# Dense expert queries taken straight from the score stage, gates multiplied in another order, and a transpose inside the RWKV inverse

## The chip, the cores and the metric

The kernel runs on one core of a Trainium2 chip. The metric is the device time of one execution in microseconds (us). The engines are named as the profile names them: PE (TensorE matmul), PEld (its weight loads), DVE (VectorE), ACT (ScalarE), POOL (GpSimd), SP (the queue that issues most DMAs).

## The reference, cut to what matters

A decoder block over 512 tokens of width 1024. After two token mixers (a gated short convolution and RWKV-7 heads) comes a product-key expert layer, PEER, in which each token picks 128 of 16,384 experts:

```python
def one_block(xb):                        # 128 tokens
    q = (xb @ wq).reshape(tb, HEADS, 2, HALF)
    s = einsum('thcd,hcnd->thcn', q, subkeys)
    sv, si = lax.top_k(s, 16)             # 16 of 128 keys, for each half
    ...                                   # 16 of the 256 sums: idx, top_s
    gate = softmax(top_s)
    hid = gelu(einsum('td,thkd->thk', xb, tab_u[idx]))
    return einsum('thk,thkd->td', gate * hid, tab_v[idx])
```

A second normalisation, a per-layer gate and a final normalisation follow. Everything is float32.

## The kernel before, in words

There are four tiles of 128 tokens, 0 to 3. A planner orders each engine's instructions by a rank (`rank(n)`, lower first) and by what is ready. Instructions given to `pin` keep the order in which the program lists them. Every engine executes its own list strictly in order.

**Group stages.** `group` runs the mixers, the query normalisation and the key scores, first for tile 0, then for tiles 1 to 3 together. Inside it, `rwkv` inverts a triangular matrix for each head. `inverse` does four heads at once in seven levels (`lv`), two chains beside each other. In a level, PE makes `Z` (L459) and `TT` (L466), DVE copies the blocks into `DT` (L468), and the transposed `Dm` is needed for the next level. At the low levels DVE transposes (L470); at the others, 32 times in all, PE multiplies `DT` by the even columns of the identity (L474) and ACT copies the 64 columns for each head into `Dm` (L476). The normalised queries of the group are written to `uq` (L226, called from `group`) and transposed for the product with `wq` (L629). For each of the 16 blocks of `wq` the weights and then a 64 KB block of subkeys `sk` are loaded on SP; `sk` has two buffers.

**Sparse tiles.** For tiles 0 and 1 each chosen expert row is fetched (POOL, `g`, 512 KB for each fetch, L768), first 128 rows of `peer_u` for the dot products (DVE, L795), then 128 rows of `peer_v` that are added to the result (DVE, L799). The rows go round in a ring of `RB = 5` buffers with the tag "g". 220 of the 256 fetches of tile 0 are spread over the group stage of tiles 1 to 3.

**Dense tiles.** For tiles 2 and 3 the kernel multiplies with all experts instead, in 128 blocks `j`. `turn_queries` makes the normalised queries again (`u2`, L226, in a buffer of the same ring "g"), PE transposes them (L892) and ACT copies them (L893). `products_of(j)` loads a block `U` (512 KB, L907) and makes 16 matmuls into PSUM (L910). `settle_block(j, gated)` applies Gelu and leaves the result in `w`. The first `J0 = 36` blocks are done with no gates. Meanwhile DVE, with POOL and ACT, selects the experts of tiles 1, 2 and 3 (`selection`, tiles `keys` and `sel`; `sel` lies in the place of `uq`). Then `Gates` turns the chosen numbers and gates (L969 to L976), and the loop over `j` from `J0` has 92 + 2 steps.

One step of that loop, in program order and all pinned: `rows_of` builds the one-hot rows of four tokens (DVE L982, L986; ACT L988 to L991); `rows(PA)` fetches and works about two sparse rows (`PA = 1.95`); `settle_block` settles block `j-1`; `joined` multiplies the one-hot rows that were built a step earlier (PE L996, into `cb`), and `placed` puts the product into `w`: blocks that are already settled are multiplied by it (DVE L1006), later ones get a copy (ACT L1008); last, `products_of(j)`. Of the 94 steps, 64 build and 64 join, spread evenly up to block `J1 = 125`. The heart of `settle_block` is

```python
if gated:
    held(act.activation(p[:, 0:gated], p[:, 0:gated], AF.Gelu_apprx_tanh))      # L919
    held(dve.tensor_tensor(w[:, 0:gated], w[:, 0:gated], p[:, 0:gated], op=OP.mult))   # L920
if gated < 256:
    held(act.activation(w[:, gated:256], p[:, gated:256], AF.Gelu_apprx_tanh))  # L922
```

**Values and end.** A last loop over 128 blocks multiplies `w` with blocks `V` of `peer_v` (PE L1073) beside the sparse rows that are left (`PB = 1.06` for each block); then come the per-layer gate and the output.

Of the kernel before, what the change touches and what calls it, by code (L numbers as in the profile page):

```python
# [9 lines left out]
F32 = mybir.dt.float32  # L10
# [5 lines left out]
AF = mybir.ActivationFunctionType  # L16
OP = mybir.AluOpType
# [3 lines left out]
T, D = 512, 1024  # L21
# [23 lines left out]
RB = 5  # L45
# [3 lines left out]
N1 = 60  # L49
N0 = 82  # L50
RA = 2.05
J0 = 36
J1 = 125
VS = 2
PA = 1.95
PB = 1.06
FIRST = 92
LEAD = 4
# [3 lines left out]
def tile_block(ctx: ExitStack, tc: tile.TileContext, x, smalls, bvec, w1, w2, wbr, wout, wq, wup, gup, subk,  # L62
               peer_u, peer_v, pT, plew, peer_ut, out, dbg=None):
    nc = tc.nc
    dve, act, pool, pe, sp = nc.vector, nc.scalar, nc.gpsimd, nc.tensor, nc.sync
# [7 lines left out]
    ring = ctx.enter_context(tc.tile_pool(name="ring", bufs=1))  # L73
# [17 lines left out]
    def rank(n):  # L91

        tc.cur_priority = int(100000 * n)
# [25 lines left out]
    ident = keep.tile([128, 128], F32, name="ident")  # L119
# [101 lines left out]
    def pin(ins):  # L221

        return tc.keep_in_program_order(ins)

    def queries_in(t, r, u):
        dve.scalar_tensor_tensor(u, hrows(t), r, gain, op0=OP.mult, op1=OP.mult)  # L226
        return u

    idx_t, gate_t, rs, ready = {}, {}, {}, []
# [13 lines left out]
    def group(tiles, wide, meanwhile=None):  # L243
        n = len(tiles)
        N = 128 * n
        stage = ExitStack()

        choice = ExitStack()
# [3 lines left out]
        wpool = stage.enter_context(tc.tile_pool(name="wpool", bufs=1, side="right", reuse_waits="tile"))  # L252
# [7 lines left out]
        def load_w(src, name, whole=wide):  # L260

            w = wpool.tile([128, KC, 128], F32, name=name, tag="w", bufs=WB[wide])
            sp.dma_start(w, src)
            if whole:
                return [w]
            place = [wpool.tile([128, KC, 128], F32R, name=f"w{q}", tag=f"w{q}", bufs=WH) for q in range(2)]
            return parts_of(w, *place)
# [42 lines left out]
        convT = big.tile([128, 4, N], F32, name="convT", tag="convT")  # L310
# [52 lines left out]
        def rwkv(i, t):  # L363
# [5 lines left out]
            p = rw_ps("d")  # L369
# [5 lines left out]
            kt = hp4("kt")  # L375
            ecol = work.tile([128, 4, 2], F32, name="ecol", tag="ecol", bufs=2)
            for hp in range(4):
                p = rw_ps("cs")
# [4 lines left out]
            a, kk, am = hp4("a"), hp4("kk"), hp4("am")  # L383
            p = rw_ps("ap")
# [6 lines left out]
            p = rw_ps("ks")  # L391
# [7 lines left out]
            p = rw_ps("rk")  # L399
# [16 lines left out]
            p = rw_ps("pb")  # L416
# [3 lines left out]
            p = rw_ps("pg")  # L420
# [4 lines left out]
            for name, src in (("b", bt), ("k", kt), ("v", v)):  # L425
                p = tr_ps("tk")
# [6 lines left out]
            for hd in range(NH):  # L433
                hp, e = divmod(hd, 2)
                q = slice(e * 64, e * 64 + 64)
                p = rw_ps("A")
# [6 lines left out]
            def inverse(g4):  # L443

                DT, Dm = hp4("DT", f"DT{g4}"), hp4("Dm", f"Dm{g4}")
                made = act.activation(DT, ident[:, None, :].to_broadcast([128, 4, 128]), AF.Copy)
                if not wide:
                    tc.keep_in_program_order(made)
                final[g4] = DT
                for lv in range(7):  # L450

                    part = lambda ap, odd: ap.rearrange("p (b two c) -> p b two c", two=2, c=1 << lv)[:, :, odd, :]
                    pairs = lambda ap, odd: ap.rearrange("p h (b two c) -> p (h b) two c", two=2, c=1 << lv)[:, :, odd, :]
                    packed = lambda p: p[:, 0:256].rearrange("p (a c) -> p a c", c=1 << lv)

                    m = 64 if lv == 6 else 128
                    p = rw_ps("Z")
                    for q in range(4):
                        pe.matmul(p[:m, q * 64:(q + 1) * 64], lhsT=AT[:, g4 * 4 + q, 3, :m], rhs=part(DT[:, q, :], 1), start=True, stop=True)  # L459
                    yield  # L460
                    if lv:
                        Z = hp4("Z", "Z", 2)[:, 0:2].rearrange("p a (b c) -> p (a b) c", c=64)
                        act.activation(Z[:m], p[:m, 0:256].rearrange("p (a b) -> p a b", b=64), AF.Copy)
                        p = rw_ps("TT")
                        for q in range(4):
                            pe.matmul(p[:m, q * 64:(q + 1) * 64], lhsT=Dm[:m, q, :m], rhs=Z[:m, q, :], start=True, stop=True)  # L466
                        yield
                    dve.copy_predicated(pairs(DT, 1)[:m], lmask[:m, lv].rearrange("p (a c) -> p a c", c=1 << lv), packed(p)[:m])  # L468
                    if lv < BLOCKT[wide]:
                        dve.transpose(flat(Dm), flat(DT))  # L470
                    elif lv < 6:
                        p = rw_ps("DD")
                        for q in range(4):
                            pe.matmul(p[:, q * 64:(q + 1) * 64], lhsT=DT[:, q, :], rhs=part(ident, 0), start=True, stop=True)  # L474
                        yield
                        act.activation(pairs(Dm, 0), packed(p), AF.Copy)  # L476


            SP = k2("SP").rearrange("p (a b) -> p a b", b=128)
# [3 lines left out]
            for hp in range(4):  # L483
                if not first:
                    pe.matmul(pH[:, hp * 128:(hp + 1) * 128], lhsT=E[:, hp, 0:128], rhs=SP[:, hp, :], start=hp == 0, stop=False, skip_group_check=True)
                for hd in (2 * hp, 2 * hp + 1):
                    c = slice(hd * 64, hd * 64 + 64)
# [156 lines left out]

        todo = None
        for b in range(16):
            w = load_w(wq[b], "wqb")
            sk = wpool.tile([128, 128], F32, name="sk", tag="sk", bufs=2)
            sp.dma_start(sk, subk[b])
            qT = qTs[b % 2]  # L650
            p = mm_ps("pq")
            product(p[:, :N], chunks(w), [lambda c, a=a: a[c] for a in uP], KC)
            act.activation(qT, p[:, :N], AF.Copy)
            if todo:
                scores(*todo)
            todo = b, sk, qT
# [96 lines left out]
        def own():  # L753
            return late.tile([128, 4 * D], F32, name="sel", tag="AT", bufs=1)

        return [Select(i, "convT" if wide else ("kt", "a", "kk")[i]) for i in range(n)], own, stage, choice


    coef_t = {}
# [80 lines left out]
        pool.tensor_scalar(half_r[t], r, 0.5, None, op0=OP.mult)  # L840


    (sel,), own, stage, choice = group([0], 1)
    sel.open(own())
    rank(0.6)
    for h0 in range(0, NH, 2):
# [12 lines left out]
        extra[0] = []  # L859

    rank(0.5)
    sels, own, stage, choice = group([1, 2, 3], 0, first_tile)
    stage.close()
    mixer_stage.close()

# [2 lines left out]
    def misc_ps(name):  # L868
        return dps.tile([128, 512], F32, name=name, tag="misc", bufs=2)
# [15 lines left out]
        return wide_w[0][:, j, :] if j < N0 else wide_w[1][:, j - N0, :]  # L885

    def turn_queries(a, t):
        u = queries_in(t, rs[t], ring.tile([128, D], F32, name="u2", tag="g", bufs=RB))
        for c4 in range(2):
            p = misc_ps("uT")  # L890
            for c in range(4):
                pe.transpose(p[:, c * 128:(c + 1) * 128], u[:, (c4 * 4 + c) * 128:(c4 * 4 + c + 1) * 128], ident)  # L892
            act.activation(uT[c4][:, :, a * 128:(a + 1) * 128], p.rearrange("p (c t) -> p c t", t=128), AF.Copy)  # L893
# [4 lines left out]
            return s_ps("S")[:, 0:256]  # L898
        return dps.tile([128, 512], F32, name="S2", tag="acc", bufs=4)[:, 0:256]

    sums = {}

    def products_of(j, fixed=False):

# [9 lines left out]
    def settle_block(j, gated, fixed=False):  # L914

        w, p = place_of_block(j), sums.pop(j)
        held = pin if fixed else lambda ins: ins
        if gated:
            held(act.activation(p[:, 0:gated], p[:, 0:gated], AF.Gelu_apprx_tanh))  # L919
            held(dve.tensor_tensor(w[:, 0:gated], w[:, 0:gated], p[:, 0:gated], op=OP.mult))  # L920
        if gated < 256:
            held(act.activation(w[:, gated:256], p[:, gated:256], AF.Gelu_apprx_tanh))  # L922

# [38 lines left out]
    class Gates:  # L962
        def __init__(self, a, t):
            self.row, self.column, self.gate, self.minus = [gain[:, (a * 4 + q) * 128:(a * 4 + q + 1) * 128] for q in range(4)]
            number, whole = As[:, a, 0], As[:, a, 1]
            ix = idx_t[t].rearrange("p h k -> p (h k)")
            p = misc_ps("pt")
            for q, (op, m) in enumerate(((OP.logical_shift_right, 7), (OP.bitwise_and, 127))):
                dve.tensor_scalar(number.bitcast(I32), ix, m, None, op0=op)  # L969
                dve.tensor_copy(whole, number.bitcast(I32))  # L970
                pin(pe.transpose(p[:, q * 128:(q + 1) * 128], whole, ident))
            pin(pe.transpose(p[:, 256:384], gate_t[t].rearrange("p h k -> p (h k)"), ident))
            pin(act.activation(self.row, p[:, 0:128], AF.Copy))
            pin(act.activation(self.column, p[:, 128:256], AF.Copy))
            pin(act.activation(self.gate, p[:, 256:384], AF.Copy))
            pin(act.activation(self.minus, p[:, 256:384], AF.Copy, scale=-1.0))  # L976
# [53 lines left out]
    built = joined = 0  # L1030
    for j in range(J0, 128 + 2):
        rank(RA + 0.0001 * j - 0.00005)
        ahead = built
        while built < 64 and built < (j - J0 + 1) * 64 / (J1 - J0):
            made[built // 32].rows_of(built % 32)
            built += 1
        if j < 128:
            rows(PA)
        if j <= 128:
            settle_block(j - 1, joined * 4, True)  # L1040
        while joined < ahead:
            a, t4 = divmod(joined, 32)
            made[a].joined(t4)
            made[a].placed(a, t4, min(j, 128))
            joined += 1
        if j < 128:
            products_of(j, True)
    assert joined == 64
# [191 lines left out]
```

## Time and profile before

| what | value |
|---|---|
| median of 3 runs | 1876.13 us (1874.98 to 1879.3) |
| the profiled execution, its own time | 1875.5 us |
| its span in the profile | 1873.6 us |
| mean granted clock of PE | 0.954 of full speed |
| busy share of the span | PE 90%, PEld 80%, DVE 76%, ACT 42%, POOL 42% |
| data moved by DMA | 499.68 MB, 267 GB/s on average |

The span is from the first to the last instruction of the profiled execution; its own time lies 1.9 us above it. Shares are averages over stages with different limits, so the stages have to be read one by one. PEclk is the share of TensorE's full clock (2.4 GHz) that was granted.

### The profile page before, as it was taken

To read this page: it belongs to the slowest core of one execution; us is meant where nothing else is said; L and a number is where in the kernel's file an instruction comes from. 1 tells how busy PE (TensorE), PEld (TensorE's weight loads), DVE (VectorE), ACT (ScalarE), POOL (GpSimd) and SP (SyncE) were. 2 spreads that over 40 slices of the span, in tenths; PEclk is the share of its full clock that TensorE was granted. 3 is DMA by queue.
4 is the path that set the end of the run, shared out by engine and by line. 5 is a ranking of instruction groups with operands and counts; after the bars stand their busy time and mean duration, and the time that the engine had idled before them with its cause. 6 is when DMAs were issued, how large, how long until landed. Compare 5 with 4: busy or idle time off the path is not lost.

```text
span 1873.6 us, 27675 instructions
## 1 busy us (share of the span) xinstructions
PE 1678.3 (90%) x9495; PEld 1496.3 (80%) x9495; DVE 1421.8 (76%) x3192; ACT 779.8 (42%) x1978; POOL 791.9 (42%) x608
## 2 busy tenths in 40 slices
PE   7999788999999878902989999999999999999997
PEld 7998787989898878902878888888887787888886
DVE  4623997777877898999951877778878899998543
ACT  4212233233222233600453776666663444454443
POOL 1000344333357554564230555555555565674000
PEclk9999989999999898956999999999999999999999
DMA  8156667555668987666454999999999999999430
GB/s 324 57 199 236 225 229 270 181 161 187 203 214 293 340 305 268 217 229 242 148 185 151 353 359 346 327 363 342 353 356 355 410 395 408 397 396 348 150 124 23
DMA packets 141857, 499.68 MB, mean 267 GB/s; under 512 B 15694, under 2 KB 20884, under 8 KB 141204
## 3 DMA queue, kind: packets, MB, share of 16 engines
q0 software_dynamic: 73728, 268.47, 40.4%
q1 hardware_dynamic: 67328, 228.09, 33.7%
q8 instruction: 75, 1.23, 0.3%
q10 hardware_dynamic: 660, 1.35, 0.2%
q14 instruction: 66, 0.54, 0.1%
HBM read 494.70 MB, written 3.15 MB: 266 GB/s over the span
## 4 chain that ended last, share of the span: by engine, by line
PE 36%; DVE 21%; issue 13%; ACT 12%; DMA 10%; POOL 7%; POOLq 0%; DVEq 0%; ACTq 0%; SPq 0%
PE acc L1073 7%; PE z L274 5%; DMA g<-in_peer_v_dram,idx 4%; POOL g L768 4%; DVE h L799 4%; PE S L910 3%; PE pg L1117 3%; DMA g<-in_peer_u_dram,idx 3%; DVE g L795 3%; PE pgate L274 2%; PE Z L459 2%; ACT h L991 2%; PE TT L466 2%; ACT near L990 2%; PE pq L274 2%
## 5 line engine op out<-in xcount | busy, mean ns | idle before, releaser
L768 POOL DMA_INDIRECT g<-in_peer_v_dram,idx x241 | 349.4, 1450 | 303.4 <-DVE h L799 222.8
L910 PE MATMUL S<-uT,U 128*128 128x256 f32 x2048 | 458.1, 382 | 6.2 <-ACT w L922 6.2
L768 POOL DMA_INDIRECT g<-in_peer_u_dram,idx x235 | 303.7, 1292 | 321.2 <-DVE g L795 257.5
L910 PEld LDWEIGHTS S<-uT,U 128*128 128x128 f32 x2048 | 386.3, 191 | 58.8 <-ACT w L922 8.2
L799 DVE SCALAR_TENSOR_TENSOR h<-g,coef,h 128x1024 f32<-128x1024 f32 x241 | 310.0, 1286 | 9.6 <-DMA g<-in_peer_v_dram,idx 8.6
L795 DVE SCALAR_TENSOR_TENSOR g<-g,u 128x1024 f32<-128x1024 f32 x235 | 284.4, 1235 | 27.8 <-DMA g<-in_peer_u_dram,idx 27.7
L1073 PE MATMUL acc<-Vh,w_parts 128*128 128x512 f32 x1024 | 286.8, 398 | 10.1 <-ACT w_parts L1065 7.7
L1073 PEld LDWEIGHTS acc<-Vh,w_parts 128*128 128x128 f32 x1024 | 193.9, 190 | 53.4 <-ACT w_parts L1065 10.6
L1073 PE MATMUL acc<-Vl,w_parts 128*128 128x512 f32 x512 | 161.4, 397 | 1.3 <-DVE Vl L1064 1.1
L1073 PEld LDWEIGHTS acc<-Vl,w_parts 128*128 128x128 f32 x512 | 96.2, 190 | 26.7 <-DVE Vl L1064 6.9
L1063 ACT ACTIVATE Vh<-V 128x1024 fp32r<-128x1024 f32 x66 | 70.0, 1061 | 96.0 <-PE acc L1073 64.5
L1064 DVE TENSOR_TENSOR Vl<-V,Vh 128x1024 fp32r<-128x1024 f32 x66 | 80.5, 1220 | 30.6 <-ACT Vh L1063 30.6
L1063 ACT ACTIVATE Vh<-h 128x1024 fp32r<-128x1024 f32 x62 | 65.9, 1062 | 90.5 <-PE acc L1073 73.2
L731 POOL TENSOR_TENSOR sel<-sel 128x800 f32<-128x800 bf16 x32 | 52.6, 1656 | 109.4 <-DVE sel L730 86.7
L922 ACT ACTIVATE w<-S 128x256 f32<-128x256 f32 (+43 forms) x124 | 37.4, 308 | 144.0 <-DVE w L920 90.3
L274 PE MATMUL z<-xh,w 128*128 128x384 f32 x416 | 88.3, 355 | 9.7 <-DVE z L326 7.4
L1064 DVE TENSOR_TENSOR Vl<-h,Vh 128x1024 fp32r<-128x1024 f32 x62 | 75.8, 1222 | 21.9 <-ACT Vh L1063 21.9
L996 PE MATMUL cb<-h 128*128 128x128 f32 x512 | 76.2, 282 | 14.8 <-ACT h L991 14.1
L996 PEld LDWEIGHTS cb<-h 128*128 128x128 f32 x512 | 69.6, 191 | 24.7 <-ACT h L991 20.6
L274 PEld LDWEIGHTS z<-xh,w 128*128 128x128 f32 x416 | 75.9, 196 | 12.5 <-DVE z L326 7.8
L892 PE MATMUL uT<-ident,u 128*128 128x128 f32 x16 | 3.8, 426 | 78.0 <-DVE u L226 78.0
L892 PEld LDWEIGHTS uT<-ident,u 128*128 128x128 f32 x16 | 3.0, 220 | 78.6 <-DVE u L226 78.2
(347 smaller groups left out, 3127.2 us busy)
## 6 DMA issues: line engine op xcount, KB each, us to landing
U<-in_peer_ut_dram SPq DMA_DIRECT2D x128, 512.0 KB, 6.5
V<-in_peer_v_dram SPq DMA_DIRECT2D x66, 512.0 KB, 5.7
h<-in_peer_v_dram SPq DMA_DIRECT2D x62, 512.0 KB, 6.7
w1b<-in_w_dram SPq DMA_DIRECT2D x52, 512.0 KB, 5.0
w2m<-in_w_dram SPq DMA_DIRECT2D x32, 512.0 KB, 4.6
wqb<-in_wq_dram SPq DMA_DIRECT2D x32, 512.0 KB, 4.7
wbr<-in_wbr_dram SPq DMA_DIRECT2D x16, 512.0 KB, 4.7
wo<-in_wout_dram SPq DMA_DIRECT2D x16, 512.0 KB, 4.5
```

The costliest lines, as they stand in the source:

```text
L274: pe.matmul(p, lhsT=a(c), rhs=b(c), start=k + c == 0, stop=(k, c) == (len(terms) - 1, n - 1))
L459: pe.matmul(p[:m, q * 64:(q + 1) * 64], lhsT=AT[:, g4 * 4 + q, 3, :m], rhs=part(DT[:, q, :], 1), start=True, stop=True)
L731: pool.tensor_tensor(hit, eq, ci[:, hd, :, None].to_broadcast([128, NCAND, 16]), op=OP.mult)
L768: fetch = pool.indirect_dma_start(out=g, out_offset=None, in_=tab, in_offset=bass.IndirectOffsetOnAxis(ap=ix[:, k:k + 1], axis=0))
L795: done = dve.scalar_tensor_tensor(g, g, 1.0, self.u, op0=OP.mult, op1=OP.mult, accum_out=self.dots[:, hd, k:k + 1])
L799: done = dve.scalar_tensor_tensor(h, g, self.cf[:, k:k + 1], h, op0=OP.mult, op1=OP.add)
L910: done = pe.matmul(p, lhsT=U[:, c * 128:(c + 1) * 128], rhs=uT[c // 4][:, c % 4, :], start=c == 0, stop=c == KC - 1)
L996: pin(pe.matmul(self.p[:, q, :], lhsT=As[:, t4 % 2, q], rhs=Bs[:, t4 % 2, q], start=True, stop=True))
L1063: pin(act.activation(Vh, V, AF.Copy))
L1064: pin(dve.tensor_tensor(Vl, V, Vh, op=OP.subtract))
L1073: pe.matmul(acc[a, dh], lhsT=w[:, a * 128:(a + 1) * 128], rhs=V[:, dh * 512:(dh + 1) * 512], start=j == 0 and q == 0, stop=j == 127 and q ...
L1117: pe.matmul(p[:, :256], lhsT=hT[:, c, :], rhs=plew_s[qd][:, c, :], start=(c == 0), stop=(c == KC - 1))
```

## The change

- `turn_queries` no longer makes the queries of tiles 2 and 3 again in a buffer of the ring "g"; PE transposes them out of `uq`, which `group` now returns.
- `J0` goes from 36 to 43, `PA` from 1.95 to 2.05. The gates are so built over blocks 43 to 125.
- In the loop, `joined` and `placed` now come ahead of `settle_block`, and `placed` treats blocks up to `j-2` as settled. The multiplication L920 is put into the list `due` and issued at the start of the next step.
- In `Gates`, the two numbers (`number`, `whole`) have a place of their own for each of the two rounds; before, the second round wrote into the place that the first transpose reads.
- In `inverse`, the product with the even columns of the identity becomes a full transpose for each head; ACT picks the even blocks of columns out of PSUM.
- `sk` has four buffers instead of two and is loaded ahead of the weights of its block.

```diff
-J0 = 36
+J0 = 43
-PA = 1.95
+PA = 2.05
...
-                            pe.matmul(p[:, q * 64:(q + 1) * 64], lhsT=DT[:, q, :], rhs=part(ident, 0), start=True, stop=True)
+                            pe.transpose(p[:, q * 128:(q + 1) * 128], DT[:, q, :], ident)
                         yield
-                        act.activation(pairs(Dm, 0), packed(p), AF.Copy)
+                        act.activation(pairs(Dm, 0), pairs(p.rearrange("p (h c) -> p h c", c=128), 0), AF.Copy)
...
+            sk = wpool.tile([128, 128], F32, name="sk", tag="sk", bufs=4)
+            sp.dma_start(sk, subk[b])
             w = load_w(wq[b], "wqb")
-            sk = wpool.tile([128, 128], F32, name="sk", tag="sk", bufs=2)
-            sp.dma_start(sk, subk[b])
...
     def turn_queries(a, t):
-        u = queries_in(t, rs[t], ring.tile([128, D], F32, name="u2", tag="g", bufs=RB))
+        u = uq[:, t - 1]
...
-            held(dve.tensor_tensor(w[:, 0:gated], w[:, 0:gated], p[:, 0:gated], op=OP.mult))
+            due.append(lambda: pin(dve.tensor_tensor(w[:, 0:gated], w[:, 0:gated], p[:, 0:gated], op=OP.mult)))
...
-            number, whole = As[:, a, 0], As[:, a, 1]
...
+                number, whole = As[:, a, q], As[:, a, 2 + q]
...
     for j in range(J0, 128 + 2):
         rank(RA + 0.0001 * j - 0.00005)
+        while due:
+            due.pop(0)()
...
-        if j <= 128:
-            settle_block(j - 1, joined * 4, True)
         while joined < ahead:
             a, t4 = divmod(joined, 32)
             made[a].joined(t4)
-            made[a].placed(a, t4, min(j, 128))
+            made[a].placed(a, t4, j - 1)
             joined += 1
+        if j <= 128:
+            settle_block(j - 1, joined * 4, True)
```

## Rows read from the trace of the kernel before

**Rows 1.** Stretches: length, busy us (PE, PEld, DVE, ACT, POOL), PEclk, DMA share, GB/s.

```profile
797.00:876.00 79.00, 0.91 (x6) 0.74 (x6) 75.82 (x191) 1.12 (x3) 51.67 (x40) 0.53 0.78 262
...
1013.70:1412.40 398.70, 383.88 (x1971) 338.68 (x1970) 309.45 (x681) 262.84 (x800) 217.52 (x170) 0.99 0.94 342
1412.40:1697.00 284.60, 273.92 (x1164) 220.54 (x1163) 268.89 (x300) 134.27 (x198) 175.59 (x108) 0.98 1.00 391
```

**Rows 2.** PE in order of time: start, us, instruction, [idle before, releaser].

```profile
876.02 3.77 PE L892 MATMUL uT<-ident,u 128*128 128x128 f32 x16 [78.01 <-DVE u L226]
879.63 69.66 PE L910 MATMUL S<-uT,U 128*128 128x256 f32 x320
...
1011.94 0.27 PE L971 MATMUL pt<-ident,h 128*128 128x128 f32 x1
```

**Rows 3.** DVE in order of time, around the end of the selections.

```profile
874.69 2.48 DVE L226 SCALAR_TENSOR_TENSOR u<-h,rs,gain 128x1024 f32<-128x1024 f32 x2
...
982.14 0.20 DVE L739 CAST idx<-sel 128x64 int32<-128x64 f32 x1
...
1012.25 0.23 DVE L970 CAST h<-h 128x128 f32<-128x128 int32 x1 [29.13 <-PE pt L971]
...
1013.32 0.43 DVE L982 TENSOR_TENSOR h<-i,gain 128x256 f32<-128x256 f32 x1
```

**Rows 4.** The issues of U on SP, and the landing of U between 797 and 880.

```profile
796.03 2.87 SPq L907 DMA_DIRECT2D U<-in_peer_ut_dram  x4
...
U<-in_peer_ut_dram SPq DMA_DIRECT2D x2, 512.0 KB, 6.1
```

**Rows 5.** DVE, ACT and PE over three steps of the gated loop.

```profile
1064.95 0.36 ACT L922 ACTIVATE w<-S 128x224 f32<-128x224 f32 x1 [0.25 <-DVE w L920]
...
1068.45 1.05 PE L996 MATMUL cb<-h 128*128 128x128 f32 x8
...
1068.97 0.36 ACT L922 ACTIVATE w<-S 128x224 f32<-128x224 f32 x1 [0.26 <-DVE w L920]
...
1069.34 3.62 PE L910 MATMUL S<-uT,U 128*128 128x256 f32 x16
1069.36 0.35 DVE L1006 TENSOR_TENSOR w<-w,cb 128x192 f32<-128x192 f32 x1 [0.42 <-ACT w L922]
1069.63 0.42 DVE L982 TENSOR_TENSOR h<-i,gain 128x256 f32<-128x256 f32 x1
1069.75 0.50 ACT L1008 ACTIVATE w<-cb 128x136 f32<-128x136 f32 x2 [0.42 <-DVE w L1006]
...
1070.14 0.40 ACT L988 ACTIVATE near<-i,gain 128x128 f32<-128x128 f32 x1
1070.48 2.60 DVE L799 SCALAR_TENSOR_TENSOR h<-g,coef,h 128x1024 f32<-128x1024 f32 x2
...
1073.48 0.18 ACT L919 ACTIVATE S<-S 128x36 f32<-128x36 f32 x1
...
1073.69 0.19 DVE L920 TENSOR_TENSOR w<-w,S 128x36 f32<-128x36 f32 x1 [0.61 <-ACT S L919]
...
1073.92 0.35 ACT L922 ACTIVATE w<-S 128x220 f32<-128x220 f32 x1 [0.26 <-DVE w L920]
...
1077.32 0.35 ACT L922 ACTIVATE w<-S 128x216 f32<-128x216 f32 x1 [2.03 <-DVE w L920]
```

**Rows 6.** Two rows of `peer_u` behind each other on DVE.

```profile
1282.57 1.21 DVE L795 SCALAR_TENSOR_TENSOR g<-g,u 128x1024 f32<-128x1024 f32 x1
...
1283.72 1.22 DVE L795 SCALAR_TENSOR_TENSOR g<-g,u 128x1024 f32<-128x1024 f32 x1
```

**Rows 7.** From the chain that ended last: four transposes, and two DD products.

```profile
328.49 0.44 PE tk L428 x4
...
357.91 1.73 PE DD L474 x16
```

**Rows 8.** The instructions on `sk`: time that PE's queue sat idle for it, times.

```profile
  DMA sk<-in_subk_dram: 8.3, 9
```

More of the change, by code (lines that the diff above doesn't have):

```diff
@@ L754, in own @@
             return late.tile([128, 4 * D], F32, name="sel", tag="AT", bufs=1)
-        return [Select(i, "convT" if wide else ("kt", "a", "kk")[i]) for i in range(n)], own, stage, choice
+        return [Select(i, "convT" if wide else ("kt", "a", "kk")[i]) for i in range(n)], own, stage, choice, uq
     coef_t = {}
@@ L840, in scale_of @@
         pool.tensor_scalar(half_r[t], r, 0.5, None, op0=OP.mult)
-    (sel,), own, stage, choice = group([0], 1)
+    (sel,), own, stage, choice, _ = group([0], 1)
     sel.open(own())
@@ L861, in tile_block @@
     rank(0.5)
-    sels, own, stage, choice = group([1, 2, 3], 0, first_tile)
+    sels, own, stage, choice, uq = group([1, 2, 3], 0, first_tile)
     stage.close()
@@ L899, in s_place @@
         return dps.tile([128, 512], F32, name="S2", tag="acc", bufs=4)[:, 0:256]
-    sums = {}
+    sums, due = {}, []
     def products_of(j, fixed=False):
@@ L964, in __init__ @@
             self.row, self.column, self.gate, self.minus = [gain[:, (a * 4 + q) * 128:(a * 4 + q + 1) * 128] for q in range(4)]
-            number, whole = As[:, a, 0], As[:, a, 1]
             ix = idx_t[t].rearrange("p h k -> p (h k)")
-            p = misc_ps("pt")
+            self.p = p = misc_ps("pt")
             for q, (op, m) in enumerate(((OP.logical_shift_right, 7), (OP.bitwise_and, 127))):
+                number, whole = As[:, a, q], As[:, a, 2 + q]
                 dve.tensor_scalar(number.bitcast(I32), ix, m, None, op0=op)
```

## The prediction

> **What bounds the kernel now.** I first read the stretches of busy time [rows 1]. From 797 to 876 us PE does almost nothing (0.91 us of 79), its granted clock is 0.53, and DVE is busy for 75.8. That is the one long hole. In the gated dense loop (1013.7 to 1412.4) PE is busy for 383.9 of 398.7 us, DVE for 309.5, ACT for 262.8, and the DMA moves 342 GB/s; in the values loop up to 1697 the DMA moves 391 GB/s and DVE is busy for 94%.
>
> PE in order of time says what the hole waits for [rows 2]: the transposes of the dense queries start at 876.02, after 78.01 us of waiting for DVE's `u` (L226). DVE makes it at 874.69 [rows 3], though the query scale was known long before. The code has the reason: `u2` takes its buffer from the ring "g", so it stands behind the 220 row fetches of tile 0, which finish there. Then PE runs its 36 blocks up to 1011.9, and DVE, which has ended the selections at 982.3, stands for 29.13 us at L970 because its place is still to be read by a transpose that PE has behind block 36 [rows 3].
>
> The third view is the gated loop step by step [rows 5]. ACT's L922 waits for DVE's L920 in each step, DVE's L1006 waits for L922, and ACT's L1008 for L1006, though they write different columns or blocks of `w`. What each pair shares is a PSUM tile, so I take it that two engines on one such tile go in program order. From one L922 to the next, a step that builds but doesn't join takes 4.02 us (1064.95 to 1068.97), one that does both 4.95, one that only joins 3.40. PE needs 3.48 for a block (20 in 69.66 [rows 2]) and 0.89 for a join (1068.45 to 1069.34). So the loop is a ring through DVE and ACT, with PE just behind it.
>
> **Start of the gated loop.** The first U loads are issued at 796.03 and land in about 6.1 us [rows 4]; that doesn't change. With `uq` there, PE can start the blocks at 802 instead of 879.6. 43 blocks of 3.48 are 150 us; the 36 before took 132.3 where 125.4 were needed, so I add the same 7 and get 959. This is before the selections end, so DVE now sets the start and the blocks are hidden behind it; that cover is 29 us wide, and only a later PE beyond it would cost.
>
> DVE's side: it loses the two `u` (-2.5 us [rows 3]). But the U stream now runs beside the rows of tile 0. These rows and the rest move 262 GB/s; a block for each 3.48 us adds 151. Together 413, against the 391 that the DMA reached in the values loop, stretches the 79 us by 4.4; against the 342 of the gated loop by 16.4. I take 5, as the 391 was moved under the same mix of queues, and keep 0 and 16. The selections so end at 982.3 - 2.5 + 5 = 984.8. The set-up is then eight small operations at 0.23 (1.8 us), which now have places of their own, and the 1.4 us from the first transpose to the first gate row (1011.94 to 1013.32): 988.0. Before it was 1013.3 [rows 3]. **-25.3** (-30 to -14).
>
> **Length of the gated loop.** Before: 64 builds over 89 steps leave 25 steps without one, so 39 steps do both, 25 only build, 25 only join, 3 neither: 39 x 4.95 + 25 x 4.02 + 25 x 3.40 + 3 x 3.48 = 389.0. The loop took 398.7, so 9.7 stay unexplained.
>
> After: 64 builds over 82 steps, so 46 do both, 18 only build, 18 only join, 3 neither. L922 no longer waits for L920, but L920 now comes after L1008, L919 and L922, and DVE has nothing else to do meanwhile: behind it are queued the next gate rows and sparse rows. From one L922 to the next, by the rows of step 1068.97 to 1073.92 [rows 5]:
>
> - Both: 0.39 (L922 to DVE's start) + 0.19 (L920) + 0.85 (L982 to L799) + 2.60 (two rows) + 0.39 (L1006 to L1008) + 0.39 (L1008 to the next on ACT) + 0.18 (L919) = 4.99. Instructions on one engine start about 0.1 before the one ahead of them ends (L988 behind L1008), twice in this sum: 4.80.
> - Only build: ACT's own work, 0.36 + 3.34 (L988 to L919) + 0.18, less 0.1: 3.80.
> - Only join: as the first without 0.85: 3.95.
>
> 46 x 4.80 + 18 x 3.80 + 18 x 3.95 + 3 x 3.48 = 370.7. Now the rest. These steps have two sparse rows each; 1.95 and 2.05 make 4.6 fewer than that before and 4.3 more after, at 1.3 us (-6.0, +5.6). And 128 of the rows are of `peer_u`, at 1.15 instead of 1.30 (1282.57 to 1283.72 [rows 6]): 19.2 us less, which counts where DVE is in the ring, 64 of 85 steps after (-14.5) and 25 of 92 before (-5.2). So the unexplained part of before is 9.7 + 6.0 + 5.2 = 20.9, or 19.3 over 85 steps. After: 370.7 + 19.3 + 5.6 - 14.5 = 381. **-17.7**. Of this, seven fewer steps at 4.33 would have given -30; the longer way of the multiplication and the denser gates give 12 back. The bounds: PE alone, 85 x 3.48 + 64 x 0.89 = 353 (-46), and whole durations instead of overlapped ones, 64 x 0.19 = 12 more (-5).
>
> **Values loop.** 179 rows were fetched in the gated loop, now 174, so five more are left over, 1.30 each: 0 if hidden, 6.5 at most. DVE and the DMA are nearly full there, but PE is too; I take **+2**.
>
> **The inverse.** Two DD products (16 instructions) take 1.73, four transposes 0.44 [rows 7]: 0.87 becomes 0.44, 32 times, 13.6 us of PE. ACT copies the same 256 columns as before, now read with gaps: no row shows a price for that, and I take none (a doubling of the copies would cost at most the gain). But DVE carries the rows of tile 0 through the same stretch and then the selections, which set the start of the gated loop; of what PE gains there I take 3 (0 to 13.6).
>
> Here the Trainium skill speaks against the change: "TensorE: Matmul & The Clock Gate", Part 4 (PE-mode transpose), gives some 275 ns for a 128 x 128 transpose inside a kernel. As time on PE, an estimate from that page makes 1.1 us of four, 0.23 longer than the products, or +7.4 us in all. The row shows 0.11 for each when they follow each other, so the figure is rather the length of one than its share of PE.
>
> **Subkeys.** PE waited 8.3 us for `sk` in all [rows 8]. The waits lie beside DVE's selection of tile 0, so I take 1 of it (0 to 8.3). Together with the inverse **-4** (-22 to 0).
>
> **Sum.** 1875.5 (the profiled execution) - 25.3 - 17.7 + 2 - 4 = 1830.5. The median of the runs is 0.6 above that execution, within their spread, so I forecast 1830.
>
> **The rivals.**
>
> - *PE sets the pace of the gated loop.* If the order of `due` hides the multiplication behind other work, the loop is PE's 353 us: 1875.5 - 25.3 - 45.7 + 2 - 4 = 1803. For it: PE is 96% busy there already. Against it: L920 has no work ahead of it on DVE that could cover the wait.
> - *The selections end later.* `sel` takes the place of `uq`, which the turned queries still read. If PE does these transposes only behind the last scores at 797, the first pieces of the selection of tile 1 go behind them; or the rows slow down by the full 16. Then the start gains only 14 us, or less if both fall together: 1842 to 1855. Against it: by the code, the transposes need only `uq` and PSUM that the mixers left long before.
> - *The deferred multiplication makes the loop slower (slower side).* If its wait, about 1.0 us from L1006 to L920's start, is added to every step of today and takes no wait away, a step is 4.33 + 1.0 and 85 of them are 453: 1875.5 - 25.3 + 54 + 2 - 4 = 1902. It decides from 4.98 us per step on (424 us), where the start's gain is eaten. For it: that wait is certain. Against it: the same reordering takes away L922's and L1006's waits of 0.2 to 2 us.
> - *A transpose takes longer in the inverse.* The turn of the dense queries took 3.77 for 16 [rows 2], 0.24 each, right behind the stretch with the clock at 0.53. At that, four take 0.94 and PE loses 32 x 0.07 = 2.3 us instead of gaining: 1830.5 + 3 + 2.3 = 1836. Against it: PE is busy without a break around the inverses. By the 275 ns of the Trainium skill's page named above it would be 1841.
> - *Nothing arrives.* If the order that the planner makes leaves the turned queries behind the selections after all, the start stays at DVE's late end and the longer steps eat the seven blocks: 1872 to 1879.
>
> **How the numbers follow.** I count a change within 0.2% (3.75 us) as none, which is about what a measurement of this kernel can tell. Forecast as described (1815 to 1850): 0.60. PE's pace: 0.13. Later selections: 0.12. Long transposes: 0.03. Faster in all: 0.88. Nothing arrives: 0.04. Slower, by the deferred multiplication: 0.08. The likeliest case gives 1830. Downward the range goes to PE's pace, 1800; upward to the later selections with whole durations in the loop, 1862. What lies outside is the slower case, most of the empty one, and the tail in which the inverse passes on all its 13.6.
>
> **What would show it.** Right: L892 with no wait for L226, the first L910 at 800 to 805, and the wait of L970 for L971 gone; PE idle for some 25 us between block 43 and the gates; the first L982 near 988; L922 no longer waiting for L920, and instead DVE's L920 waiting for ACT's L922 in most steps, by 0.7 to 1 us; the gated loop at 4.4 to 4.5 us a step; L474 half as long. Wrong: L718 or L730 of tile 1 waiting for L892, a landing of the rows of tile 0 far above 6 us, or a step near 4.15 (PE) or 5 (the ring).

## The result and the profile after

The changed kernel takes 1848.3 us (median of four runs, 1843.86 to 1850.83) beside 1875.56 for the kernel before: ratio 0.9849 with a 95% interval of 0.9823 to 0.9876, so 27 us faster. The forecast was 1830 with a range of 1800 to 1862. The sign and the range held; 18 us of the forecast gain are missing.

The profiled execution after took 1843.86 us, 31.6 less than the one before. PE splits it into three stretches: the first matmul behind the gates' transposes starts at 991.66 instead of 1013.68 (-22.0), the gated loop from there to the end of block 127 takes 389.3 instead of 402.2 (-12.9), and the rest takes 3.3 more. Executions of one kernel differ by up to 17 us here, so I take verdicts from medians and ratios, and mechanisms from profiles.

PE in order of time, after (start, us, instruction, idle before it and what ended that; answers to [rows 2]):

```profile
772.20 1.04 PE L892 MATMUL uT<-ident,uq 128*128 128x128 f32 x8
773.49 1.15 PE L892 MATMUL uT<-ident,uq 128*128 128x128 f32 x8 [0.25 <-ACT uT L893]
777.26 22.64 PE L910 MATMUL S<-uT,U 128*128 128x256 f32 x96 [2.62 <-DMA U<-in_peer_ut_dram]
819.97 9.80 PE L910 MATMUL S<-uT,U 128*128 128x256 f32 x32 [20.07 <-ACT w L922]
836.84 16.80 PE L910 MATMUL S<-uT,U 128*128 128x256 f32 x64 [7.07 <-ACT w L922]
...
881.11 13.40 PE L910 MATMUL S<-uT,U 128*128 128x256 f32 x48 [7.53 <-ACT w L922]
...
949.47 41.71 PE L910 MATMUL S<-uT,U 128*128 128x256 f32 x192 [3.15 <-ACT w L922]
991.01 0.38 PE L971 MATMUL pt<-ident,h 128*128 128x128 f32 x2
```

The 78 us wait for `u` is gone, as forecast, and the scores end earlier too: 772.2 instead of 798.0. But the 43 blocks, which I had put at 157 us, take 213.7, from 777.26 to 991.0. After six of them (96 matmuls) PE stops for 20 us, and then seven more times, always for ACT's L922: 49.1 us in all. The matmuls between the stops take 164.8 us, 15 more than 43 x 3.48.

Part of those 15 is in the granted clock. Stretches of the trace after (length, busy us of PE, PEld, DVE, ACT and POOL with the instructions, PEclk, DMA share, GB/s; answers to [rows 1]):

```profile
800.00:820.00 20.00, 0.03 (x1) 0.03 (x1) 17.77 (x34) 1.75 (x3) 12.56 (x11) 0.62 0.99 374
820.00:949.00 129.00, 100.43 (x400) 83.82 (x400) 110.55 (x611) 62.63 (x289) 36.18 (x24) 0.86 0.33 110
949.00:991.00 42.00, 41.53 (x192) 36.55 (x193) 6.00 (x13) 6.00 (x18) 7.23 (x7) 1.00 0.60 201
```

The granted clock, here a mean over its two levels of 1.2 and 2.4 GHz, is at 0.62 while PE stands and at 0.86 over the stretch with the later stops; at the 1.00 of the third line, 12 blocks take 41.7 us, 3.48 each. How much of the 15 us the clock makes up, no run shows.

What ACT waited for at the first stop stands in its own order of time and in DVE's (after; the last two DVE lines answer to [rows 3]):

```profile
818.24 1.28 ACT L922 ACT_TABLE_LOAD   x1 [42.97 <-DVE h L799]
819.53 0.66 ACT L922 ACTIVATE w<-S 128x256 f32<-128x256 f32 x2
```

```profile
816.83 1.26 DVE L799 SCALAR_TENSOR_TENSOR h<-gx,coef,h 128x1024 f32<-128x1024 f32 x1
...
961.24 0.19 DVE L739 CAST idx<-sel 128x64 int32<-128x64 f32 x1
...
991.85 0.43 DVE L982 TENSOR_TENSOR h<-i,gain 128x256 f32<-128x256 f32 x1 [29.75 <-ACT gain L973]
```

`gx` is an extra row buffer that `first_tile` lends to the ring for the rows of tile 0. By the order in which the code opens and closes its pools, it lies in memory that the dense weights `w0` take over; e5 tests this. The first Gelu writes `w0`, so it waits for the last row that DVE works out of `gx`, at 818.09. Before the change this could not show: PE itself started only behind those rows. And DVE, done with the selections at 961.4 (982.3 before), stands for 29.75 us for the gates, whose transposes are queued on PE behind block 43. PE sets the start, not DVE.

The gated loop, DVE's L920 and ACT's L919 and L922 (after; answers to [rows 5]):

```profile
1005.64 0.16 DVE L920 TENSOR_TENSOR w<-w,S 128x8 f32<-128x8 f32 x1 [1.06 <-ACT w L922]
...
1010.47 0.17 DVE L920 TENSOR_TENSOR w<-w,S 128x12 f32<-128x12 f32 x1 [1.05 <-ACT w L922]
...
1014.46 0.17 DVE L920 TENSOR_TENSOR w<-w,S 128x16 f32<-128x16 f32 x1 [1.05 <-ACT w L922]
...
1018.26 0.17 DVE L920 TENSOR_TENSOR w<-w,S 128x16 f32<-128x16 f32 x1 [0.27 <-ACT w L922]
```

```profile
1009.45 0.51 ACT L1008 ACTIVATE w<-cb 128x148 f32<-128x148 f32 x2 [0.52 <-DVE w L1006]
1009.84 0.19 ACT L919 ACTIVATE S<-S 128x12 f32<-128x12 f32 x1
1010.06 0.37 ACT L922 ACTIVATE w<-S 128x244 f32<-128x244 f32 x1
```

This is the ring of the prediction: a step that builds and joins takes 4.83 us (1005.64 to 1010.47; forecast 4.80), one that only joins 3.99 (3.95), one that only builds 3.80 (3.80); the medians over the whole loop are 4.88, 4.02 and 3.80. L920 stands at the head of each, waiting for L922 behind L1008 and L919.

### The profile page after: what moved, and what is told of

Same layout as the page of the kernel before. It is cut to its first block, busy times and chain, and to the rows that moved or that the text cites. A ratio compares the mean times of both kernels' runs of the same rounds, so it can differ in the third digit from the quotient of the medians.

```text
span 1842.1 us, 27396 instructions
## 1 busy us (share of the span) xinstructions
PE 1666.9 (90%) x9367; PEld 1478.9 (80%) x9367; DVE 1415.4 (77%) x3186; ACT 780.9 (42%) x1971; POOL 809.5 (44%) x608
## 4 chain that ended last, share of the span: by engine, by line
PE 34%; DVE 23%; issue 15%; DMA 10%; POOL 9%; ACT 7%; POOLq 0%; DVEq 0%; ACTq 0%; SPq 0%
PE acc L1075 9%; POOL g L768 6%; DMA g<-in_peer_v_dram,idx 5%; DVE h L799 4%; PE z L274 4%; DVE g L795 4%; PE pg L1119 3%; PE pgate L274 3%; DMA g<-in_peer_u_dram,idx 3%; PE S L910 2%; PE Z L459 2%; PE TT L466 2%; DVE w L257 2%; PE pbr L274 1%; DVE sel L736 1%
## 5 line engine op out<-in xcount | busy, mean ns | idle before, releaser
L910 PE MATMUL S<-uT,U 128*128 128x256 f32 x2048 | 470.5, 388 | 51.7 <-ACT w L922 49.1
L768 POOL DMA_INDIRECT g<-in_peer_v_dram,idx x241 | 360.9, 1497 | 291.9 <-DVE h L799 216.7
L910 PEld LDWEIGHTS S<-uT,U 128*128 128x128 f32 x2048 | 394.1, 195 | 108.9 <-ACT w L922 52.6
L768 POOL DMA_INDIRECT g<-in_peer_u_dram,idx x235 | 311.3, 1325 | 291.5 <-DVE g L795 229.6
L1075 PE MATMUL acc<-Vh,w_parts 128*128 128x512 f32 x1024 | 286.2, 397 | 12.5 <-ACT w_parts L1067 9.2
L920 DVE TENSOR_TENSOR w<-w,S 128x256 f32<-128x256 f32 (+40 forms) x85 | 25.0, 295 | 65.9 <-ACT w L922 62.6
L1008 ACT ACTIVATE w<-cb 128x152 f32<-128x152 f32 (+35 forms) x95 | 22.4, 269 | 105.7 <-DVE w L1006 102.7
L991 ACT ACTIVATE h<-near,gain 128x128 f32<-128x128 f32 x128 | 63.1, 493 | 4.2
```

What stands on the lines that cost most here:

```text
L768: fetch = pool.indirect_dma_start(out=g, out_offset=None, in_=tab, in_offset=bass.IndirectOffsetOnAxis(ap=ix[:, k:k + 1], axis=0))
L910: done = pe.matmul(p, lhsT=U[:, c * 128:(c + 1) * 128], rhs=uT[c // 4][:, c % 4, :], start=c == 0, stop=c == KC - 1)
L991: pin(act.activation(B[:, q], near, AF.Relu, scale=of(self.minus), bias=of(self.gate)))
L1075: pe.matmul(acc[a, dh], lhsT=w[:, a * 128:(a + 1) * 128], rhs=V[:, dh * 512:(dh + 1) * 512], start=j == 0 and q == 0, stop=j == 127 and q ...
```

## The experiments

The instants below are read from each kernel's own trace: the end of the last score product (where PE goes on to the dense queries or stops), the first matmul of the blocks (L910), the first behind the gates, the end of block 127, and the execution's own time; the gated loop is the difference of the third and the fourth. In e4, e5, e8 and e11 these lines stand two further down (L912).

| kernel | scores end | first block | behind the gates | block 127 ends | loop | own time | median |
|---|---|---|---|---|---|---|---|
| before | 798.0 | 879.6 | 1013.7 | 1415.9 | 402.2 | 1875.5 | 1875.6 |
| after | 772.2 | 777.3 | 991.7 | 1381.0 | 389.3 | 1843.9 | 1848.3 |
| e1 before, transposes | 779.2 | 860.2 | 994.2 | 1393.5 | 399.3 | 1855.2 | 1860.8 |
| e2 before, subkeys | 793.2 | 874.7 | 1010.5 | 1412.5 | 402.1 | 1871.6 | 1868.3 |
| e3 before, queries | 792.7 | 798.8 | 991.8 | 1390.6 | 398.8 | 1849.9 | 1852.5 |
| e4 e3 without late `gx` | 795.8 | 800.6 | 989.1 | 1390.9 | 401.7 | 1848.6 | 1850.6 |
| e5 after without late `gx` | 778.6 | 783.5 | 971.3 | 1360.4 | 389.1 | 1819.5 | 1828.3 |
| e6 after, L920 later | 776.4 | 781.9 | 999.4 | 1364.0 | 364.7 | 1826.6 | 1826.6 |
| e7 after, old order | 775.6 | 780.9 | 995.4 | 1380.6 | 385.2 | 1843.2 | 1848.9 |
| e8 both of e5 and e6 | 776.8 | 782.1 | 971.5 | 1337.3 | 365.8 | 1796.6 | 1800.9 |
| e9 after, 36 blocks | 780.6 | 785.6 | 979.2 | 1384.7 | 405.5 | 1845.1 | 1844.0 |
| e10 after, products | 790.3 | 795.3 | 1010.0 | 1399.4 | 389.5 | 1865.7 | 1866.3 |
| e11 e8, fewer rows ahead | 776.4 | 781.9 | 957.3 | 1345.6 | 388.3 | 1808.5 | 1809.1 |

Ratios to the kernel before on the same chip, with 95% intervals: e1 0.9934 (0.9919 to 0.9949), e2 0.9979 (0.9964 to 0.9995), e3 0.9892 (0.9877 to 0.9906), e4 0.9882 (0.9867 to 0.9896), e5 0.974 (0.9692 to 0.9789), e6 0.9728 (0.9679 to 0.9777), e7 0.9862 (0.9801 to 0.9924), e8 0.9599 (0.9551 to 0.9647), e9 0.981 (0.9769 to 0.985), e10 0.9941 (0.9918 to 0.9964), e11 0.9651 (0.9606 to 0.9695).

### e1 and e10: the transposes of the inverse, alone and taken out

e1 is the kernel before with

```diff
-  pe.matmul(p[:, q * 64:(q + 1) * 64], lhsT=DT[:, q, :], rhs=part(ident, 0), start=True, stop=True)
+  pe.transpose(p[:, q * 128:(q + 1) * 128], DT[:, q, :], ident)
-  act.activation(pairs(Dm, 0), packed(p), AF.Copy)
+  act.activation(pairs(Dm, 0), pairs(p.rearrange("p (h c) -> p h c", c=128), 0), AF.Copy)
```

and e10 the changed kernel with this edit reversed.

> The kernel before with one edit alone, the inverse turned by transposes. The prediction's step (PE gains 13.6 us, DVE keeps 10 of them, 3 arrive): 1872, the last score product no more than 4 us earlier than 798, the selections ending within 3 us of 982. The rival, formed on the trace of the changed kernel, where the last score product ends 25.8 us earlier: each inverse is a chain of PE and ACT that the next piece of DVE waits for, so DVE gains what the chain loses; then the last score product ends at 775 to 785, the selections end 13 to 20 us earlier and the time is 1855 to 1862.

> The changed kernel with the products of before in the inverse. The prediction's step: 3 us of the transposes' 13.6 arrive, so taking them out costs 3: 1851. The rival (all of it arrives, in the changed kernel as in the one before): 1858 to 1865, and the last score product some 13 to 19 us later than in the changed kernel.

e1 is 12 to 13 us faster than before, e10 18 slower than the changed kernel, and their scores end 18.8 us earlier and 18.1 us later. The ends of the scores are from one execution each, and these scatter: in the changed kernel, e6, e7 and e9, whose edits all lie behind the scores, they are at 772.2 to 780.6. The times alone say that the edit brings about all of PE's 13.6 us, where I took 3; whether it brings more stays open. PE's instructions on `DD` before and in e1 (duration in ns, minimum, median, maximum):

```profile
L474 PE MATMUL DD<-ident,DT x256: 217/275/276, 92.7 to 555.0; 128*128 128x64 f32 x128
```

```profile
L474 PE MATMUL DD<-ident,DT x128: 270/272/319, 88.7 to 536.8; 128*128 128x128 f32 x128
```

Half as many instructions, each no longer. ACT's copy with gaps takes 384 ns as before. I had argued that DVE, full of rows of tile 0, would keep the gain. One stretch of the trace before and DVE's waits from 250 to 700 us (us, times, longest), before and in e1, say otherwise:

```profile
400.00:550.00 150.00, 146.99 (x1069) 135.15 (x1068) 118.47 (x216) 46.81 (x113) 57.38 (x48) 1.00 0.59 188
```

```profile
DVE DT L468 <- PE TT L466: 31.0, 29, 3.0
```

```profile
DVE DT L468 <- PE TT L466: 19.3, 23, 2.1
```

PE is busy for 147 of 150 us and DVE for 118; DVE stands in the inverse for PE's `TT`, so what PE gains there DVE gains too. It was a stretch that I had not read.

### e2: the subkeys alone

```diff
+  sk = wpool.tile([128, 128], F32, name="sk", tag="sk", bufs=4)
+  sp.dma_start(sk, subk[b])
   w = load_w(wq[b], "wqb")
-  sk = wpool.tile([128, 128], F32, name="sk", tag="sk", bufs=2)
-  sp.dma_start(sk, subk[b])
```

> The kernel before with one edit alone, the subkeys loaded ahead of the query weights and from four buffers. The prediction's step: 1 of the 8.3 us of waiting arrives, 1874.5. The rival, formed on the trace of the changed kernel, where the scores of tile 0 end 11 us earlier but the next projection only 3.5: 3 to 8 us arrive, 1867 to 1872.

0.9979 is 3.9 us (1 to 7). The rival fits better: about half of the 8.3 us of [rows 8] arrives, though the interval reaches down to the 1 us of the prediction.

### e3 and e4: the queries alone, and the extra buffer

e3 is the kernel before with `u = uq[:, t - 1]` in `turn_queries` (36 blocks). e4 adds, in `first_tile`, with `turn` for the rank of row `k`:

```diff
-  sparse[0].all(range(128 + K0), turn)
+  sparse[0].all(range(128 + K0 - 40), turn)
   extra[0] = []
+  sparse[0].all(range(128 + K0 - 40, 128 + K0), turn)
```

> The kernel before with one edit alone, the dense queries turned from those of the scores; 36 blocks ahead of the gates as before. The prediction's step (the selections set the start, PE is hidden): the wait of DVE for PE ahead of the gates is gone, the first gate row at 983 to 989, 1846 to 1851. The rival: the first Gelu waits for the last row of tile 0 that was worked on in the extra ring buffer, six blocks fill PSUM and PE stops for some 20 us and again behind ACT's selection work, so that its 36 blocks end near 990 and the first gate row is at 991 to 996, with DVE still waiting for PE there: 1853 to 1858.

> The last kernel (queries alone) with the extra ring buffer left alone by the last 40 of the 220 rows of tile 0, so that the place of the dense weights is free early. If that buffer holds up the first Gelu: its wait falls from some 40 us to under 8, PE's 36 blocks end 15 to 25 us earlier than in the run beside it, and the selections set the start; 4 to 9 us faster than that run if PE had set it there, the same within 2 if DVE had. The rival (ACT's order, with the selection's accumulations ahead of the Gelus, stops PE all the same): the blocks end within 5 us of the run beside it.

PE in order of time, e3 and then e4:

```profile
798.80 22.36 PE L910 MATMUL S<-uT,U 128*128 128x256 f32 x96 [3.69 <-DMA U<-in_peer_ut_dram]
840.26 10.01 PE L910 MATMUL S<-uT,U 128*128 128x256 f32 x32 [19.10 <-ACT w L922]
...
990.04 0.27 PE L971 MATMUL pt<-ident,h 128*128 128x128 f32 x1
```

```profile
800.63 95.17 PE L912 MATMUL S<-uT,U 128*128 128x256 f32 x432 [2.36 <-DMA U<-in_peer_ut_dram]
907.65 12.24 PE L912 MATMUL S<-uT,U 128*128 128x256 f32 x48 [11.86 <-ACT w L924]
...
987.87 0.45 PE L973 MATMUL pt<-ident,h 128*128 128x128 f32 x1 [11.19 <-DVE h L972]
```

In e3 the rival holds: PE stops for 19.10 us after six blocks, and the first gate row is at 991.4; the time of 1852.5 lies just below the 1853 put down for it. Without the late rows in `gx` (e4), 27 blocks run without a stop where six did, and PE is done with all 36 at 943.6, 46 us earlier than in e3, where 15 to 25 were expected. Yet the time is the same within 2 us: now PE waits for DVE's selections, which end at 987.2 (981.7 in e3), about where PE ended in e3. In e4 the cover that the prediction assumed exists, and DVE's first gate row, forecast at 988.0, is at 988.50 (e4):

```profile
988.50 0.42 DVE L984 TENSOR_TENSOR h<-i,gain 128x256 f32<-128x256 f32 x1
```

Two smaller errors cancel there: the selections end 2.4 later than the 984.8 that I had, and the way from them to the gate row takes 1.3 us instead of 3.2.

### e5: the changed kernel with the same edit of the extra buffer

> The changed kernel with the extra ring buffer left alone by the last 40 of the 220 rows of tile 0. Theory (the first Gelu waits 43 us because its output lies where that buffer is still in use, PSUM fills and PE stops for 20 us): the stall at 800 to 820 is gone, the 43 blocks end near 970, the first gate row moves from 991.9 to 967 to 975 and the time from 1848 to 1825 to 1832. The rival (ACT works in order, and its selection work stops PE at the next place): the blocks end no more than 5 us earlier, 1842 to 1848. A cost of the edit itself, the last 40 rows with one buffer less, would show as DVE waiting longer for their landing: up to 5 us.

20 us faster, as the theory has it. PE, and ACT at the next stop (e5):

```profile
783.48 93.48 PE L912 MATMUL S<-uT,U 128*128 128x256 f32 x432 [2.44 <-DMA U<-in_peer_ut_dram]
890.16 12.62 PE L912 MATMUL S<-uT,U 128*128 128x256 f32 x48 [13.20 <-ACT w L924]
...
970.63 0.66 PE L973 MATMUL pt<-ident,h 128*128 128x128 f32 x2 [3.41 <-DVE h L972]
```

```profile
888.23 0.29 ACT L734 ACTIVATE sel<-sel 128x50 f32<-128x50 f32 x1 [31.57 <-POOL sel L731]
...
889.74 0.36 ACT L924 ACTIVATE w<-S 128x256 f32<-128x256 f32 x1
```

The 43 blocks take 183.2 us instead of 213.7: 21 us less of waiting (28.0 instead of 49.1) and 9 less in the matmuls themselves. The stop that is left is the rival's: ACT, in order, stands at a selection piece that waits for POOL, with Gelus behind it. By then DVE is the later one by 3.4 us. The cost that the edit might have had does not show: between 700 and 960 us DVE waits 6.9 us for rows to land, in the changed kernel 7.6.

### e6 and e7: where L920 stands in the step

e6 moves `while due: due.pop(0)()` from the head of the step to behind `rows(PA)`. e7 puts back the order of before:

```diff
-  due.append(lambda: pin(dve.tensor_tensor(w[:, 0:gated], ...)))
+  held(dve.tensor_tensor(w[:, 0:gated], ...))
...
+  if j <= 128:
+      settle_block(j - 1, joined * 4, True)
   while joined < ahead:
       ...
-      made[a].placed(a, t4, j - 1)
+      made[a].placed(a, t4, min(j, 128))
-  if j <= 128:
-      settle_block(j - 1, joined * 4, True)
```

> The changed kernel with the deferred multiplications issued behind the step's sparse rows instead of at its start. Theory (DVE waits about 1 us in each of 64 joining steps for the Gelu of the step before, in a ring through DVE and ACT): the wait of L920 for L922, 63 us in all, falls under 20, a joining step takes 4.0 to 4.3 instead of 4.84, and the gated loop shortens from 389 to 360 to 370: 1820 to 1830. The rival (the wait moves to the join behind it, because DVE and ACT take turns on its PSUM tile too): the loop stays within 5 us, 1843 to 1850.

> The changed kernel with the order of the kernel before in each step (Gelu, its multiplication at once, then the join); 43 blocks and the rest as in the changed one. By the prediction's sum, both orders make steps of about the same mean length (371.8 against 370.7 us for 85 steps) and the order is worth under 5 us either way: 1843 to 1853. The rival: the reordering itself brought the gain of the loop, and without it the loop is back near 399 us: 1856 to 1860. The other rival: the deferred multiplication costs, as one of the prediction's rivals had it, and without it the loop is at 375 or less: below 1836.

e7 is where the changed kernel is: the order as made is worth nothing (the loop, by its profile, is even 4 us shorter in the old one), and all of the loop's gain comes from the seven steps less. e9 agrees: with the new order and the 36 blocks and rows of before, the loop takes 405.5 us beside 402.2. e6, with the same instructions and L920 some 2.6 us later in DVE's list, takes 24.6 us off the loop and 22 off the time. What DVE waited for ahead of L920, after and then in e6 (us, times):

```profile
  ACT w L922: 62.6, 74
```

```profile
  ACT w L922: 0.9, 2
```

DVE in two steps of e6:

```profile
1046.21 0.18 DVE L920 TENSOR_TENSOR w<-w,S 128x32 f32<-128x32 f32 x1
1046.31 0.37 DVE L1006 TENSOR_TENSOR w<-w,cb 128x212 f32<-128x212 f32 x1
...
1049.98 0.18 DVE L920 TENSOR_TENSOR w<-w,S 128x36 f32<-128x36 f32 x1
1050.63 0.38 DVE L1006 TENSOR_TENSOR w<-w,cb 128x216 f32<-128x216 f32 x1 [0.47 <-PE cb L996]
```

DVE works its two sparse rows while ACT does L919 and L922, and the join that follows waits for PE, if for anything. The ring is open. The Trainium skill ("PSUM — Partial Sum Buffer", section "PSUM bank collisions raise a hardware error") says why such a wait is there though the two write different columns: two engines may not touch one bank at the same time. The trace agrees in that L920 and L922, on one PSUM tile, never overlap in it.

### e8: both edits, and e11: fewer rows ahead of the gates

> The changed kernel with both edits, the extra ring buffer left alone at the end and the deferred multiplications behind the sparse rows. If the two causes are apart (one sets the start of the gated loop, one its length), the gains add: 1848 less the gain of either alone, within 5 us; if both theories hold, 1797 to 1812. If PE is the next bound of the loop, its mean step is no shorter than 4.15 us, which the prediction worked out for PE alone.

The gains add: 20.0 and 21.7 alone, 47.4 together, a little beyond the 5 us allowed. At 1800.9 us this is the fastest kernel of the study, 4.0% below the one before. Its first matmul behind the gates is e5's, its loop e6's.

e11 sets `K0 = 76` instead of 92 and `PA = 2.25` in e8:

> The version with both edits (the extra ring buffer left alone at the end, the multiplications behind the sparse rows: 1801) with 16 of the 220 rows of tile 0 moved into the gated loop (2.25 a step instead of 2.05), where DVE is busy for 301 of 365 us. If DVE's selections set the start there by the 5 us that PE waits for them: first gate row 5 us earlier, the loop unchanged, 1793 to 1798. The rival: 17 more rows a step beside the U stream put the DMA at its limit (0.95 busy there already) or DVE back in the ring, the loop grows by 5 us or more: 1801 to 1810.

A miss for the theory, 8 us slower by the medians, inside the rival's range. The start comes 14 us earlier, but the loop grows by 22.5. The DMA from 1000 to 1320 us, e8 and then e11:

```profile
DMA packets 32169, 117.39 MB, mean 367 GB/s; under 512 B 3568, under 2 KB 3568, under 8 KB 32140
```

```profile
DMA packets 32233, 117.57 MB, mean 367 GB/s; under 512 B 3585, under 2 KB 3585, under 8 KB 32206
```

Both move the same 367 GB/s, and at that rate 17 more rows of 0.524 MB take 24 us, so a limit of the DMA in this mix would fit. But DVE's own work fits as well, as the stretch of the gated loop shows, e8 and then e11 (columns as in [rows 1]):

```profile
971.50:1337.30 365.80, 356.70 (x1874) 318.28 (x1872) 301.89 (x673) 256.78 (x784) 211.57 (x168) 0.99 0.95 359
```

```profile
957.30:1345.60 388.30, 365.07 (x1874) 321.93 (x1872) 323.62 (x691) 258.93 (x788) 234.21 (x185) 0.98 0.96 362
```

DVE is busy for 21.7 us more, nearly the 22.5 by which the loop grows, and stands for 64 us in both; of these, its waits for rows that have not landed grow only from 32 to 39. In neither loop does PE ever wait for a block `U`. In e8 it is busy for 356.7 of 365.8 us, 4.20 a step, and stands for only 9 us, at joins behind ACT's L993 (L991 in the changed kernel). So e8's loop is close to PE's pace, of which 4.15 was worked out, and e11's rows slow it again, by DVE's work or by the DMA. No run varied the one without the other.

### e9: 36 blocks in the changed kernel

`J0 = 36`, `PA = 1.95` in the changed kernel.

> The changed kernel with 36 blocks ahead of the gates and 1.95 sparse rows a step, as before. The prediction's step: PE's blocks ahead of the gates are hidden behind DVE, so taking seven of them back brings the start nothing (first gate row stays at 989 to 992) and the loop grows by some 13 us to 400: 1858 to 1864. The rival, formed on the trace (PE sets the start): seven blocks less bring the first gate row forward by 7 x 3.48 = 24 us, to where DVE's selections end (962 to 970), and the loop gives 13 back: 1834 to 1841, faster than with 43.

Not slower, as the prediction's step would have it, and by the median 4 us faster, which the intervals do not separate from none. The rival's mechanism holds, its size only in part. The first matmul behind the gates comes 12.5 us earlier, though the scores end 8.4 later in this execution, and the loop gives back 16.2. DVE still waits there for PE, but no longer by 29.75 us (e9):

```profile
979.37 0.42 DVE L982 TENSOR_TENSOR h<-i,gain 128x256 f32<-128x256 f32 x1 [7.24 <-ACT gain L973]
```

## Why the prediction was right, and where it was not

- **The queries from `uq`: right.** L892 waits for nothing but the scores, and the first block starts behind a 2.6 us wait for U. This edit alone is worth 20 us (e3).
- **"The blocks are hidden behind DVE; that cover is 29 us wide": this step failed.** I took the same 7 us of stops for 43 blocks as for the 36 of before. But those ran behind all but one of the rows of tile 0 and beside 80 of ACT's 128 selection pieces (L734); in the new place 27 of these rows are still ahead of DVE, and all 128 pieces stand beside the blocks. The stops came to 49.1 us and a lower clock added some more, so the blocks needed 213.7 instead of 157. They ended 30 us after the selections, and the cover became its opposite. e5 shows the largest part to be the late rows in `gx`; e4 shows that with that cover DVE does set the start, and at about the instant that I had worked out. That the start still came out 22.0 us earlier, near the forecast of 25.3, is luck: it took a gain in the inverse that I had not forecast. In e10, which lacks that gain, the blocks behind the gates begin at 1010.0, only 3.7 us earlier than before the change.
- **The inverse and the subkeys: right in sign, mis-sized.** Forecast -4, measured -13 and -4 alone (e1, e2). The error was to call DVE the bound of a stretch that PE bounds. It hid the other error: without those 17 us, PE would have ended its blocks later still. Alone, the transposes, the subkeys and the queries bring 12, 4 and 20 us (e1 to e3), together more than the 27 of the whole change. The rival of longer transposes fell: 272 ns is the duration of one, close to the 275 ns that the Trainium skill gives for bfloat16 inside a kernel ("TensorE: Matmul & The Clock Gate", Part 4: PE-mode transpose), but the products had that duration too, and twice as many instructions.
- **Length of the loop: mechanism right, -12.9 instead of -17.7.** The three kinds of step came out within 0.04 us in the steps shown, within 0.08 as medians over the loop. With those shown the steps sum to 46 x 4.83 + 18 x 3.80 + 18 x 3.99 + 3 x 3.48 = 372.8, so the rest that I carried over from before is 16.5 us and not 10.4. Half of this difference is a slip of mine: the 398.7 us that I took for the loop before stop at 1412.4, where block 127 starts, and the 402.2 of the table where it ends. With 402.2 the rest of before is 24.4, scaled 22.5, and after the change 13.6; the forecast would have been 384.3, still 17.9 shorter, and 5.0 short of the 389.3. I scaled the rest without asking what it was. The trace has waits of DVE that no kind of step contains (after, 991.66 to 1381; us, times, longest):

```profile
DVE coef L818 <- ACT q L817: 11.3, 5, 2.3
DVE h L799 <- DMA g<-in_peer_v_dram,idx: 3.1, 3, 1.3
DVE g L795 <- DMA g<-in_peer_u_dram,idx: 2.1, 3, 1.7
```

L817 is the Gelu of 16 finished dot products, which ACT reaches only behind its gate rows; the other two lines are rows that had not landed. Together they are 16.5 us, in a few steps of 5 to 7 us. The agreement with the rest is not exact, as other parts of the steps changed too. That the order is a wash (371.8 against 370.7) is what e7 shows.
- **Seven blocks ahead of the gates**, counted as free, are not: they cost PE about what they save in the loop (e9).
- **Values loop:** +2 forecast; the rest of the kernel takes 3.3 more.
- **The rivals.** PE's pace in the loop did not come, since L920 kept the ring closed; e6, which opens it, reaches 4.29 a step. The multiplication deferred to the step's head did cost a certain wait, as the slower rival said, but took others away, so the time is the same; the loop itself is some 4 us longer for it (e7).

Not settled: what of the transposes' gain goes beyond PE's own 13.6 us (e1 and e10 give 13 and 18), and what the waits for L817 cost, since no run took them out. The places of their own that `Gates` gives its numbers were not tested alone either.

## What to carry to other kernels

Work that is moved into an earlier gap meets what else lived there: ask of each of its outputs which memory it is written to and who still uses that place, and of each engine on its way (here ACT) what stands ahead in its list. A cover holds only when the hidden work is costed in its new place. An instruction that must wait for another engine belongs behind work of its own engine that is as long as the wait: one move of L920 by two sparse rows was worth 22 us, more than the whole reordering around it.

## What was not expected of the hardware

- With the U stream and the rows of both tables, two loops with a different number of rows moved 367 GB/s alike (e8, e11), while the values loop of e8, from 1380 to 1620 us, moved 399.
- After the 20 us in which PE stood, the granted clock was 0.86 on average over the next 129 us with short stops: 0.73 in the first 9.8 us of work behind the long stop, 1.00 in the 14.1 us of work from 859.51, 0.79 behind the next stop of 7.53 us. In the last 42 us, in which PE did not stop again, it was 1.00.
